# Feed-forward networks with nine paired blocks instead of eight, and way down's sums added to x by DMAs

## The chip, the cores and the metric

The kernel runs on one core of a Trainium2 chip. The metric is device time in microseconds (us), from a run of the whole program on that core; a smaller number is better. The span in a profile goes from the first to the last instruction of the program.

## The reference

One layer of a transformer: two feed-forward networks (FFNs) with a mixer of two kinds of attention between them, on 512 tokens of width 1024, all in float32.

```python
def rmsnorm(x, g):
    xf = x.astype(jnp.float32)
    y = xf * lax.rsqrt(jnp.mean(xf * xf, axis=-1, keepdims=True) + RMS_EPS)
    return (y * g.astype(jnp.float32)).astype(x.dtype)

def swiglu(h, w_gate, w_up, w_down):
    return (jax.nn.silu(h @ w_gate) * (h @ w_up)) @ w_down

def reference(x, ...):
    for l in range(DEPTH):          # DEPTH = 1
        x = x + 0.5 * swiglu(rmsnorm(x, norm_ffn1[l]), w_ffn1_gate[l], w_ffn1_up[l], w_ffn1_down[l])
        x = x + hybrid_mixer(rmsnorm(x, norm_mix[l]), ...)
        x = x + 0.5 * swiglu(rmsnorm(x, norm_ffn2[l]), w_ffn2_gate[l], w_ffn2_up[l], w_ffn2_down[l])
    return rmsnorm(x, norm_final)
```

The FFN's inner width is 2816, that is 22 blocks of 128 features.

## The kernel before

**Layout and precision.** x is kept transposed: xs[0] to xs[7], each 128 model rows by 512 tokens. TensorE (PE) takes every operand as two halves, hi and lo, whose sum is the float32 value: ACT copies the value into the rounded type (hi), DVE subtracts (lo). A product is three matmuls, hi hi, hi lo and lo hi (`mm3`, lines 93 to 95), summed in PSUM.

**An FFN.** Each of the 22 feature blocks needs gate and up (1024 x 128 each, times x) and gives a tile h = silu(gate) * up, again in halves (`kept`). Way down then multiplies the h tiles and adds half of the sum to xs[d], for the eight d.

- *Plain blocks* (`plain`), the first PLAIN = 6: the norm's gain is in x's halves (`gained`, tiles xo), 1/rms is not; R holds 1/rms as a 128 x 512 tile, and `finish` multiplies both sums by it. In three-block groups, the first half of x's rows (j = 0) comes for all blocks before the second.
- *Pairs* (`pair`), the other 16 blocks as 8 pairs: one Strassen-like scheme with seven products instead of eight, on halves of the tokens (HT = 256 columns) and of x's rows. Its operands on x's side are the blocks B11, B21, B22 and the sums T1 to T4, which `sums_of_x` and `blocks_of_x` form from x times gain times R while the plain blocks run; on the weights' side A11, A12, A22 and the sums S1 to S4 (DVE). Banks: u in tag s, v in t, w in o. When its last product ends, a closure (`c11`, `c12`, `c22`, `c21`) adds the banks, applies silu and keeps h.
- *Way down* (`down`) is cut into steps of three matmuls, called fills; its sums lie in the PSUM banks of tag mm (two of them). When a sum is complete, `half_added` (DVE, line 485) adds half of it to xs[d]. The h blocks form parts: the six plain ones, then fours. The fills of a part are mixed into the pair steps of the next part (`mixed`); the first LEAD = 12 fills of the plain part come at once after the plain blocks (`begun`).

**Order of the work.** `go` writes out PE's order by hand. A step has a cost, and loads, sums and halves are issued when PE is 26.0, 12.8 and 8.6 us of such cost away. The closures of a product are issued one step late. The other engines' orders, and PE's outside of `go` and of the mixer, are a planner's. Weights come in 512 KB loads on the SP queue: `raw` (three buffers) for plain blocks and way down, `aw` (six) for pairs; split weights are in sph and spl (three each).

**Beginning and end.** Twelve matmuls on ones (`wake`) run before the data are there. The first weight block is loaded in pieces and split at columns 2, 4 and 8. After the second FFN's pairs, `turn_x` transposes x (PE: px), first xs[0] to xs[3] for the four token blocks, then xs[4] to xs[7]; the last part's way down is formed per token block with h as the weights, and the final norm follows.

**The mixer** has its own order by hand; projections (pp) use the mm banks, logits (ps_s) the s banks. A small product, ps_c, comes four times and takes an mm bank.

Of the kernel before, what the change touches and what calls it, by code (L numbers as in the profile page):

```python
# [9 lines left out]
F32 = mybir.dt.float32  # L10
# [5 lines left out]
S = 512  # L16
# [5 lines left out]
FP = 4  # L22
PLAIN = 6
# [5 lines left out]
LEAD = 12  # L29
# [3 lines left out]
def block_kernel(ctx: ExitStack, tc: tile.TileContext, A: dict, out: bass.AP):  # L33
# [140 lines left out]

    class Ffn:


        def __init__(self, w, which, tmp, hp, sp):
            self.w, self.which, self.tmp, self.hp, self.sp = w, which, tmp, hp, sp
            self.xg, self.hs, self.early, self.cuts = None, {}, {}, ()  # L180
            self.b, self.temps = {}, {}
# [3 lines left out]
        def two(self, k):  # L185
            return [self.sp.tile([128, 2, 4, 128], F32, name=n, tag=t, bufs=3).rearrange("p a b c -> p (a b c)")
                    for n, t in (("xa", "sph"), ("xb", "spl"))]

        def sums_of_x(self, k):
            ac, bd = self.two(k)  # L190
            a, c, b, d = ac[:, :S], ac[:, S:S + HT], bd[:, :S], bd[:, S:]
            for t, i in ((a, k), (b, k + 4)):
                nc.vector.scalar_tensor_tensor(t, xs[i], gcol[:, self.which, i:i + 1], R, ALU.mult, ALU.mult)
            nc.vector.tensor_tensor(c, a[:, :HT], a[:, HT:], ALU.subtract)
            nc.vector.scalar_tensor_tensor(d[:, HT:], c, -1.0, b[:, HT:], ALU.mult, ALU.subtract)
            nc.vector.scalar_tensor_tensor(d[:, :HT], d[:, HT:], -1.0, b[:, :HT], ALU.mult, ALU.subtract)
            nc.vector.tensor_tensor(a[:, HT:], b[:, HT:], a[:, HT:], ALU.subtract)
            self.halves_of_x(self.th[:, k, 0:2], self.tl[:, k, 0:2], d.rearrange("p (a b) -> p a b", a=2))
            self.halves_of_x(self.th[:, k, 2], self.tl[:, k, 2], a[:, HT:])
            self.temps[k] = a[:, :HT], b, c  # L200
# [5 lines left out]
        def blocks_of_x(self, k):  # L206
            a, b, c = self.temps.pop(k)
            for i in (k, k + 4):
                self.b[i] = [xp.tile([128, S], F32R, name="xo", tag="xo", bufs=20) for _ in range(2)]
            hi, lo = self.b[k]  # L210
            self.halves_of_x(hi[:, :HT], lo[:, :HT], a)
            self.halves_of_x(hi[:, HT:], lo[:, HT:], c)
            self.halves_of_x(*self.b[k + 4], b)

        def moving(self, name):

            first, second = slice(0, HT), slice(HT, S)
            k, cols = {"B11": (0, first), "T1": (0, second), "B21": (4, first), "B22": (4, second)}.get(
                name, (None, None))
            if cols:  # L220
                return [(self.b[i][0][:, cols], self.b[i][1][:, cols]) for i in range(k, k + 4)]
            n = ("T4", "T2", "T3").index(name)
            return [(self.th[:, i, n], self.tl[:, i, n]) for i in range(4)]
# [4 lines left out]
        def kept(self, f, h):  # L228

            hi, lo = [self.hp.tile([128, S], F32R, name="h", tag="h", bufs=16) for _ in range(2)]  # L230
            nc.scalar.activation(hi, h, AF.Copy)
            nc.vector.tensor_tensor(lo, h, f32(hi), ALU.subtract)
            self.hs[f] = hi, lo

        def raw(self):
            return self.sp.tile([128, 2, 4, 128], F32, name="aw", tag="aw", bufs=6)

        def split(self, v):

            hi, lo = [self.sp.tile([128, 2, 4, 128], F32R, name=n, tag=n, bufs=3) for n in ("sph", "spl")]  # L240
            self.halves_of_x(hi, lo, v)
            return hi, lo

        def plain(self, fs):
# [3 lines left out]
            def loads(f, j):  # L248
                if (f, j) in self.early:
                    A[f, j] = self.early.pop((f, j))  # L250
                    return
                A[f, j] = chunk((8, 128))
                nc.sync.dma_start(A[f, j], self.w[f][:, j].rearrange("p a b c -> p (a b) c"))

            def halves_of(f, j):
                half[f, j] = halves(A.pop((f, j)), (2, 4, 8) if (f, j) in self.cuts else (8,))

            def run(f, j, m):
                if j == 0:
                    bank[f, m] = pt(("s", "t", "o", "mm")[(2 * f + m) % 4], "pgu")  # L260
                for k in range(4):
                    mm3(bank[f, m], half[f, j][4 * m + k], self.xg[4 * j + k], j == k == 0, j == 1 and k == 3)
# [16 lines left out]
        def pair(self, f):  # L279
# [3 lines left out]
            def loads(j):  # L283
                for i in range(2):
                    A[i, j] = self.raw()
                    nc.sync.dma_start(A[i, j], self.w[f + i][:, j])

            def sums(name):
# [4 lines left out]
                nc.vector.tensor_tensor(to, x, y, op)  # L293
# [7 lines left out]
            def run(m, n, to, a, b, first):  # L301
# [4 lines left out]
                for k, x in list(enumerate(self.moving(b)))[2 * n:2 * n + 2]:  # L306
                    mm3(bank[to][:, m], (hi[:, m, k], lo[:, m, k]), x, first and m == k == 0, k == 3, True)
# [16 lines left out]
            def c22():  # L324
                t = out[1] = self.t()
                nc.vector.tensor_tensor(t[:, :, HT:], bank["u"], part["w1"], ALU.add)
                nc.scalar.activation(t[:, 0, HT:], t[:, 0, HT:], AF.Silu, scale=-1.0)
                nc.vector.scalar_tensor_tensor(t[:, 1, HT:], t[:, 1, HT:], -1.0, t[:, 0, HT:], ALU.mult, ALU.mult)
# [58 lines left out]
        def mixed(self, steps, fills):  # L387

            out, done = [], 0
            ends, inner = range(5, len(steps) - 1, 2), range(6, len(steps) - 2, 2)  # L390
            more = max(0, len(fills) - len(ends))
            taken = set(ends[:len(fills)]) | {inner[(2 * n + 1) * len(inner) // (2 * more)] for n in range(more)}
            for i, s in enumerate(steps):
                out.append(s)
                if i in taken:
                    out.append(fills[done])
                    done += 1
            return out + fills[done:]
# [33 lines left out]
    def begun(ffn, w, first, posts):  # L432

        steps = [s for f in range(0, PLAIN, 3) for s in ffn.plain(range(f, f + 3))]
        sums = [(first + 2 * k, lambda k=k: ffn.sums_of_x(k)) for k in range(4)]
        blocks = [(at, lambda k=k: ffn.blocks_of_x(k)) for k, at in enumerate((first, 18, 18, 23))]
        for at, post in posts + sums + blocks:
            steps[at].post.append(post)
        fills = ffn.down(w, range(PLAIN), half_added, "mm", 2)
        return steps + fills[:LEAD], fills[LEAD:]  # L440

# [44 lines left out]

    with ExitStack() as ph:
# [6 lines left out]
        for _ in range(12):  # L494
# [5 lines left out]
        for f in range(3):  # L500
# [12 lines left out]
        first_w(0, [slice(0, 2)], nc.scalar)  # L513
        first_w(0, [slice(2, 4)], nc.sync)
# [5 lines left out]
        first_w(2, [slice(0, 8)], nc.sync)  # L520
# [8 lines left out]
        ffn.xg = [gained(k, 0) for k in range(NK)]  # L529

# [20 lines left out]
        def then(d, p):  # L551
# [4 lines left out]
        steps, fills = begun(ffn, A["wd1"], 6, [  # L556
            (3, squares_of_tokens), (4, lambda: roots(0, ss[:, 0])), (5, lambda: rows_of_roots(0, "mm")),
            (12, make_rows)])
        pairs = []
        for f in range(PLAIN, NF, FP):  # L560
            fs = range(f, f + FP)
            own = [step for i in fs[::2] for step in ffn.pair(i)]
            pairs += own
            steps += ffn.mixed(own, fills)
            if fs[-1] < NF - 1:
                fills = ffn.down(A["wd1"][f:], fs, half_added)
            else:
                steps += ffn.down(A["wd1"][f:], fs, then, None, 4)
        pairs[36].post.append(put_rows)
# [6 lines left out]
    with ExitStack() as ph:  # L576
# [411 lines left out]
        def cmp_pair(pair):  # L988
# [4 lines left out]
            def logits():  # L993
                need("kc")
                s = pt("mm", "ps_c")
# [140 lines left out]
    with ExitStack() as ph:  # L1136
# [7 lines left out]
        steps, fills = begun(ffn, A["wd2a"], 5, [  # L1144
            (2, lambda: roots(2, sums_of_squares("mm"))), (4, lambda: rows_of_roots(2, "mm"))])
        for f in range(PLAIN, NF, FP):
            fs = range(f, f + FP)
            steps += ffn.mixed([step for i in fs[::2] for step in ffn.pair(i)], fills)
            if fs[-1] < NF - 1:
                fills = ffn.down(A["wd2a"][f:], fs, half_added)  # L1150
        ffn.go(steps)
# [31 lines left out]
        last = range(NF - FP, NF)  # L1183
        w = []
        for half in range(2):
# [3 lines left out]
            hi, lo = [t.rearrange("p a b c -> p (a b c)") for t in ffn.split(v.rearrange("p (a b c) -> p a b c", a=2, b=4))]  # L1189
# [40 lines left out]
def _gate_up(gate, up):  # L1230
# [3 lines left out]
    return np.ascontiguousarray(v.transpose(4, 3, 1, 0, 2, 5))  # L1234


def _down(w):
# [4 lines left out]
    for f, end in zip((0, *range(PLAIN, NF, FP)), (*range(PLAIN, NF + 1, FP),)):  # L1242
# [5 lines left out]
def _laid_out(x, norm_ffn1, w_ffn1_gate, w_ffn1_up, w_ffn1_down, norm_mix, w_in, cmp_pos_k, cmp_w1_k,  # L1248
# [24 lines left out]
        "wd2a": _down(w_ffn2_down[0])[:NF - FP],  # L1273
        "wd2b": _blocks(w_ffn2_down[0][F - FP * 128:], FP * 128, S),
# [27 lines left out]
```

## Time and profile before

| | |
|---|---|
| median of 3 runs | 986.14 us (984.13 to 986.63) |
| profiled execution | 982.87 us, its span 981.0 us |
| granted TensorE clock, mean | 0.998 |
| PE, DVE, ACT, POOL busy | 970.0, 702.2, 499.0, 168.9 us |
| DMA | 113.86 MB, mean 116 GB/s |
| first FFN: first product starts, plain blocks end | 6.79, 74.23 us |
| second FFN: plain blocks end, pairs end | 695.5, 948.5 us |

A row of a group of instructions reads: line, engine, operation, tile written <- tiles read, shapes, count | busy us, mean ns of one | idle time of the engine before them, and what ended it. A timeline row reads: start us, duration us, engine, line, operation, tiles, shapes, count, and in brackets the idle time before it. A row of waits reads: who waited for whom: us in total, times, longest. A row of a stretch reads: from:to, its length, then busy time (and count) of PE, weight loads, DVE, ACT and POOL, granted clock, DMA share, GB/s. Matmuls overlap in the rows: the time of one is read from start to start.

### The profile page before, as it was taken

What the parts mean: (1) busy time and instruction counts of PE and PEld (TensorE: products, weight loads), DVE (VectorE), ACT (ScalarE), POOL (GpSimd) and SP (SyncE); (2) the same over time, 40 slices, a digit from 0 to 9 for tenths busy, and PEclk for the clock granted to TensorE, in tenths of its full rate; (3) what the DMA queues carried; (4) which work ended last, traced back from release to release, by engine and by line L of the source; (5) the groups of instructions that cost most, each with busy time, mean ns of one, the idle gap of its engine ahead of it and who ended that gap; (6) DMA issues with size and microseconds to landing.
All of it is one profiled execution on the core that took longest, in us unless ns stands there. A gap on an engine that the chain in (4) does not pass through costs nothing.

```text
span 981.0 us, 15636 instructions
## 1 busy us (share of the span) xinstructions
PE 970.0 (99%) x5944; PEld 857.6 (87%) x5944; DVE 702.2 (72%) x1118; ACT 499.0 (51%) x853; POOL 168.9 (17%) x297
## 2 busy tenths in 40 slices
PE   9999999999999999999999999999999999999997
PEld 7888989999999898888888888888899999999995
DVE  4996576878676475668878885688765777767653
ACT  7654344444434345577666674645443434434444
POOL 0000000000000144256566564800000000000002
PEclk9999999999999999999999999999999999999999
DMA  9633247332321135662233531543333233342102
GB/s 328 220 111 123 79 155 204 106 125 86 109 86 42 46 103 155 213 182 74 61 102 97 130 98 54 194 171 107 97 119 129 84 97 100 108 130 93 37 1 86
DMA packets 45742, 113.86 MB, mean 116 GB/s; under 512 B 10049, under 2 KB 14866, under 8 KB 45668
## 3 DMA queue, kind: packets, MB, share of 16 engines
q1 hardware_dynamic: 45380, 112.73, 37.0%
q8 instruction: 47, 0.77, 0.3%
q14 instruction: 27, 0.22, 0.1%
q10 hardware_dynamic: 288, 0.14, 0.1%
HBM read 100.08 MB, written 5.30 MB: 107 GB/s over the span
## 4 chain that ended last, share of the span: by engine, by line
PE 93%; DMA 2%; POOL 1%; DVE 1%; issue 1%; SPq 1%; ACT 0%; DVEq 0%; ACTq 0%; POOLq 0%
PE pd L94 8%; PE pd L95 8%; PE pd L93 8%; PE pu L93 6%; PE pu L95 6%; PE pu L94 6%; PE pw L93 4%; PE pw L95 4%; PE pw L94 4%; PE pgu L94 4%; PE pgu L95 4%; PE pgu L93 4%; PE pv L93 3%; PE pv L95 3%; PE pv L94 3%; PE pp L93 3%
## 5 line engine op out<-in xcount | busy, mean ns | idle before, releaser
L203 ACT ACTIVATE sph<-aw 128x1024 fp32r<-128x1024 f32 x114 | 121.0, 1061 | 222.5 <-PE pu L94 112.7
L81 ACT ACTIVATE whi<-raw 128x1024 fp32r<-128x1024 f32 (+3 forms) x115 | 112.2, 978 | 124.1 <-PE pd L94 50.4
L204 DVE TENSOR_TENSOR spl<-aw,sph 128x1024 fp32r<-128x1024 f32 x114 | 139.2, 1221 | 43.3 <-ACT sph L203 43.2
L88 DVE TENSOR_TENSOR wlo<-raw,whi 128x1024 fp32r<-128x1024 f32 (+3 forms) x90 | 111.2, 1237 | 37.5 <-ACT whi L81 36.6
L94 PE MATMUL pd<-h,whi 128*128 128x512 f32 x320 | 126.7, 396 | 0.0
L93 PE MATMUL pd<-h,whi 128*128 128x512 f32 x320 | 126.1, 394 | 0.0
L95 PE MATMUL pd<-h,wlo 128*128 128x512 f32 x320 | 125.8, 393 | 0.0
L95 PE MATMUL pu<-th,spl 128*128 128x256 f32 x384 | 106.2, 277 | 0.0
L93 PE MATMUL pu<-th,sph 128*128 128x256 f32 x384 | 106.1, 276 | 0.0
L293 DVE TENSOR_TENSOR aw<-aw 128x1024 f32<-128x1024 f32 x64 | 78.1, 1220 | 39.0 <-DMA aw<-in_wgu 32.3
L94 PE MATMUL pu<-tl,sph 128*128 128x256 f32 x384 | 106.0, 276 | 0.0
L93 PEld LDWEIGHTS pu<-th,sph 128*128 128x128 f32 x384 | 72.1, 188 | 6.4 <-issue 0.5
L94 PEld LDWEIGHTS pu<-tl,sph 128*128 128x128 f32 x384 | 72.1, 188 | 5.5
L93 PE MATMUL pgu<-xo,whi 128*128 128x512 f32 x192 | 75.4, 393 | 0.0
L94 PE MATMUL pgu<-xo,whi 128*128 128x512 f32 x192 | 74.9, 390 | 0.3 <-DVE xo L130 0.3
L95 PE MATMUL pgu<-xo,wlo 128*128 128x512 f32 x192 | 74.8, 389 | 0.0
L86 POOL TENSOR_TENSOR wlo<-raw,whi 128x128 fp32r<-128x128 f32 x136 | 64.1, 505 | 57.3 <-ACT whi L81 29.2
L95 PEld LDWEIGHTS pu<-th,spl 128*128 128x128 f32 x384 | 72.1, 188 | 0.0
L95 PEld LDWEIGHTS pd<-h,wlo 128*128 128x128 f32 x320 | 60.1, 188 | 13.4
L95 PE MATMUL pw<-xo,spl 128*128 128x256 f32 x256 | 70.8, 277 | 0.0
L93 PE MATMUL pw<-xo,sph 128*128 128x256 f32 x256 | 70.7, 276 | 0.0
L94 PE MATMUL pw<-xo,sph 128*128 128x256 f32 x256 | 70.7, 276 | 0.0
(253 smaller groups left out, 2423.0 us busy)
## 6 DMA issues: line engine op xcount, KB each, us to landing
aw<-in_wgu SPq DMA_DIRECT2D x64, 512.0 KB, 3.8
raw<-in_wgu SPq DMA_DIRECT2D x23, 512.0 KB, 5.3
raw<-in_wd SPq DMA_DIRECT2D x22, 512.0 KB, 3.5
raw<-in_wd2a SPq DMA_DIRECT2D x18, 512.0 KB, 3.6
raw<-in_w_a SPq DMA_DIRECT2D x16, 512.0 KB, 3.6
raw<-in_w SPq DMA_DIRECT2D x8, 512.0 KB, 3.9
kvn<-xo SPq DMA_DIRECT2D x32, 128.0 KB, 2.4
aq<-xo SPq DMA_DIRECT2D x32, 128.0 KB, 2.4
```

The costliest lines, as they stand in the source:

```text
L81: nc.scalar.activation(hi[:, s], src[:, s], AF.Copy)
L86: nc.gpsimd.tensor_tensor(lo[:, i, b], src[:, i, b], f32(hi[:, i, b]), ALU.subtract)
L88: nc.vector.tensor_tensor(lo[:, s], src[:, s], f32(hi[:, s]), ALU.subtract)
L93: nc.tensor.matmul(p, w[0], v[0], start=first, stop=False, skip_group_check=again)
L94: nc.tensor.matmul(p, w[0], v[1], start=False, stop=False, skip_group_check=again)
L95: nc.tensor.matmul(p, w[1], v[0], start=False, stop=last, skip_group_check=again)
L203: nc.scalar.activation(hi, v, AF.Copy)
L204: nc.vector.tensor_tensor(lo, v, f32(hi), ALU.subtract)
L293: nc.vector.tensor_tensor(to, x, y, op)
```

## The change

1. PLAIN = 4: four plain blocks in groups of two, then nine pairs. Parts of way down: 0-3, 4-5, 6-9, 10-13, 14-17, 18-21.
2. Pairs take x with its gain but without 1/rms: the blocks B are the plain blocks' own halves xo, `blocks_of_x` goes, and `sums_of_x` forms the T from x times gain (two ACT copies per row pair, four DVE operations, then halves). R multiplies the finished products: one DVE operation of 128 x 1024 in `c12` and one in `c21`; `c21` first copies its bank.
3. `half_sent` replaces `half_added` for all parts but the plain one, and there for odd d: ACT copies half of the sum to acc (one tile), and a DMA issued by POOL adds acc to xs[d].
4. `mixed`: a fill follows pair step i if i modulo 28 is in SLOTS (16 of 28) and the fill's part is at least six steps old; what is over comes after the last pair. LEAD = 10.
5. First block: gate and up of a 128-row piece are adjacent in memory and, for the block loaded in pieces, in PE's order; its first load is four columns on SP, a third early block is not loaded; 8 matmuls of wake instead of 12.
6. Order on the other engines: pair loads behind the last plain load on SP, sums S behind the last lo of h on DVE, the scaled x behind the last xo or h on ACT; the plain blocks' halves at high priority.
7. In the mixer, ps_c takes an s bank instead of an mm bank.

```diff
-FP = 4
-PLAIN = 6
+PLAIN = 4
+PARTS = (0, 4, 6, 10, 14, 18, 22)
-LEAD = 12
+LEAD = 10
+SLOTS = (0, 1, 2, 3, 4, 5, 6, 7, 9, 12, 15, 18, 21, 23, 25, 27)
...
         def sums_of_x(self, k):
...
-            for t, i in ((a, k), (b, k + 4)):
-                nc.vector.scalar_tensor_tensor(t, xs[i], gcol[:, self.which, i:i + 1], R, ALU.mult, ALU.mult)
...
+            with after(self.behind):
+                for n, i in enumerate((k, k + 4)):
+                    nc.scalar.activation(ab[:, n * S:(n + 1) * S], xs[i], AF.Copy, scale=gcol[:, self.which, i:i + 1])
+            a1, a2, b1, b2 = [ab[:, i * HT:(i + 1) * HT] for i in range(4)]
+            t4, t2, t3, t1 = [v[:, i] for i in range(4)]
+            nc.vector.tensor_tensor(t1, a1, a2, ALU.subtract)
+            nc.vector.scalar_tensor_tensor(t2, t1, -1.0, b2, ALU.mult, ALU.subtract)
+            nc.vector.scalar_tensor_tensor(t4, t2, -1.0, b1, ALU.mult, ALU.subtract)
+            nc.vector.tensor_tensor(t3, b2, a2, ALU.subtract)
+            self.halves_of_x(self.th[:, k], self.tl[:, k], v[:, :3])
...
-        def blocks_of_x(self, k):
...
+            def run(f, j, at):
+                both = (f, j) in self.cuts
+                order = [(k, m) for k in range(2 * at, 2 * at + 2) for m in range(2)] if both else [
+                    (k, at) for k in range(4)]
...
             def c12():
...
+                nc.vector.tensor_tensor(t, t, R.unsqueeze(1).to_broadcast([128, 2, S]), ALU.mult)
...
             def c21():
                 t = out[1]
-                nc.scalar.activation(t[:, 0, :HT], bank["u"][:, 0], AF.Silu, scale=-1.0)
-                nc.vector.scalar_tensor_tensor(t[:, 1, :HT], bank["u"][:, 1], -1.0, t[:, 0, :HT], ALU.mult, ALU.mult)
+                nc.scalar.activation(t[:, :, :HT], bank["u"], AF.Copy)
+                nc.vector.tensor_tensor(t, t, R.unsqueeze(1).to_broadcast([128, 2, S]), ALU.mult)
+                nc.scalar.activation(t[:, 0], t[:, 0], AF.Silu, scale=-1.0)
+                nc.vector.scalar_tensor_tensor(t[:, 1], t[:, 1], -1.0, t[:, 0], ALU.mult, ALU.mult)
                 self.kept(f + 1, t[:, 1])
...
         def mixed(self, steps, fills):
...
+                if i % 28 in SLOTS and fills and fills[0][0] <= i:
+                    out.append(fills.pop(0)[1])
+            return out + [fill for _, fill in fills]
...
+        steps = [s for f in range(0, PLAIN, 2) for s in ffn.plain(range(f, f + 2))]
+        sums = [(at, lambda k=k: ffn.sums_of_x(k)) for k, at in enumerate((3, 7, 9, 11))]
...
+        fills = ffn.down(w, range(PLAIN), lambda d, p: (half_sent if d % 2 else half_added)(d, p), "mm", 2)
+        return steps + fills[:LEAD], [(0, step) for step in fills[LEAD:]]
...
+    def half_sent(d, p):
+        nc.scalar.activation(acc, p, AF.Copy, scale=0.5)
+        nc.gpsimd.dma_start(xs[d], acc, accum_op=ALU.add)
...
-        for _ in range(12):
+        for _ in range(8):
...
         first_x(0)
-        first_w(0, [slice(0, 2)], nc.scalar)
-        first_w(0, [slice(2, 4)], nc.sync)
+        first_w(0, [slice(0, 4)], nc.sync)
         first_x(1)
...
-        first_w(2, [slice(0, 8)], nc.sync)
...
+        for f, end in zip(PARTS[1:], PARTS[2:]):
+            fs = range(f, end)
+            pairs += [step for i in fs[::2] for step in ffn.pair(i)]
+            if end < NF:
+                fills += [(len(pairs) + 6, step) for step in ffn.down(A["wd1"][f:], fs, half_sent)]
+        steps += ffn.mixed(pairs, fills) + ffn.down(A["wd1"][f:], fs, then, None, 4)
...
-                s = pt("mm", "ps_c")
+                s = pt("s", "ps_c")
```

The second FFN is put together as the first, without the group of four at its end.

More of the change, by code (lines that the diff above doesn't have):

```diff
@@ L173, in __init__, with after @@
             self.ahead, self.post = (loads, sums, halves), []
+    def after(ins):
+        return tc.issue_after(ins.ins if hasattr(ins, "ins") else ins)
     class Ffn:
@@ L180, in __init__ @@
             self.xg, self.hs, self.early, self.cuts = None, {}, {}, ()
[L181 removed]
+            self.behind = made[0]
+            self.t1 = [[xp.tile([128, S], F32R, name="xo", tag="xo", bufs=20) for _ in range(2)] for _ in range(2)]
             self.th, self.tl = [sp.tile([128, 4, 3, HT], F32R, name=n, tag=n, bufs=1) for n in ("th3", "tl3")]
             nc.gpsimd.memset(sp.tile([128, 16], F32, name="gap", tag="gap", bufs=1), 0.0)
[L185 to L187 removed]
@@ L197, in sums_of_x @@
[L197 to L200, printed above, removed]
+            ab, v = [self.sp.tile([128, 4, 2, 128], F32, name=n, tag=t, bufs=3).rearrange("p a b c -> p (a b c)")
+                     for n, t in (("xa", "sph"), ("xv", "spl"))]
+            v = v.rearrange("p (a b) -> p a b", a=4)
@@ L204, in halves_of_x @@
             nc.vector.tensor_tensor(lo, v, f32(hi), ALU.subtract)
-        def blocks_of_x(self, k):
[L207 to L213, printed above, removed]
-        def moving(self, name):
[L217 to L223, printed above, removed]
+        def moving(self, name):
+            if name == "T1":
+                return [[h[:, k % 2 * HT:(k % 2 + 1) * HT] for h in self.t1[k // 2]] for k in range(4)]
+            if name[0] == "T":
+                n = ("T4", "T2", "T3").index(name)
+                return [(self.th[:, i, n], self.tl[:, i, n]) for i in range(4)]
+            k, c = {"B11": (0, 0), "B21": (4, 0), "B22": (4, 1)}[name]
+            cols = slice(c * HT, (c + 1) * HT)
+            return [(self.xg[i][0][:, cols], self.xg[i][1][:, cols]) for i in range(k, k + 4)]
         def t(self):
@@ L252, in loads @@
                 A[f, j] = chunk((8, 128))
-                nc.sync.dma_start(A[f, j], self.w[f][:, j].rearrange("p a b c -> p (a b) c"))
+                self.behind_load = nc.sync.dma_start(A[f, j], self.w[f][:, j].rearrange("p a b c -> p (a b) c"))
             def halves_of(f, j):
[L256 to L262, printed above, removed]
+                with tc.high_priority():
+                    half[f, j] = halves(A.pop((f, j)), (2, 4, 8) if (f, j) in self.cuts else (8,))
+            def run(f, j, at):
+                both = (f, j) in self.cuts
+                order = [(k, m) for k in range(2 * at, 2 * at + 2) for m in range(2)] if both else [
+                    (k, at) for k in range(4)]
+                for k, m in order:
+                    if j == k == 0:
+                        bank[f, m] = pt(("s", "t", "o", "mm")[(2 * f + m) % 4], "pgu")
+                    mm3(bank[f, m], half[f, j][2 * k + m], self.xg[4 * j + k], j == k == 0, j == 1 and k == 3)
             def finish(f):
@@ L387, in mixed @@
         def mixed(self, steps, fills):
[L389 to L392, printed above, removed]
+            out, fills = [], list(fills)
             for i, s in enumerate(steps):
                 out.append(s)
[L395 to L398, printed above, removed]
+                if i % 28 in SLOTS and fills and fills[0][0] <= i:
+                    out.append(fills.pop(0)[1])
+            return out + [fill for _, fill in fills]
         def go(self, steps):
@@ L429, in go, with begun @@
                     late()
[L432 to L437, printed above, removed]
+    def begun(ffn, w, posts):
+        steps = [s for f in range(0, PLAIN, 2) for s in ffn.plain(range(f, f + 2))]
+        sums = [(at, lambda k=k: ffn.sums_of_x(k)) for k, at in enumerate((3, 7, 9, 11))]
+        for at, post in posts + sums:
             steps[at].post.append(post)
-        fills = ffn.down(w, range(PLAIN), half_added, "mm", 2)
-        return steps + fills[:LEAD], fills[LEAD:]
+        fills = ffn.down(w, range(PLAIN), lambda d, p: (half_sent if d % 2 else half_added)(d, p), "mm", 2)
+        return steps + fills[:LEAD], [(0, step) for step in fills[LEAD:]]
     scr_t = dp.tile([16, 128, RVW], F32, name="scr_t")
@@ L529, in block_kernel @@
         ffn.xg = [gained(k, 0) for k in range(NK)]
+        ffn.behind = made[0]
         def squares_of_tokens():
@@ L554, in then @@
             squares(tmp, d, "tmp", 3)
-        steps, fills = begun(ffn, A["wd1"], 6, [
+        steps, fills = begun(ffn, A["wd1"], [
             (3, squares_of_tokens), (4, lambda: roots(0, ss[:, 0])), (5, lambda: rows_of_roots(0, "mm")),
-            (12, make_rows)])
+            (13, make_rows)])
         pairs = []
[L560 to L569, printed above, removed]
+        for f, end in zip(PARTS[1:], PARTS[2:]):
[4 more added lines that the diff above has]
+        steps += ffn.mixed(pairs, fills) + ffn.down(A["wd1"][f:], fs, then, None, 4)
+        pairs[20].post.append(put_rows)
         for i in range(8):
@@ L1142, in block_kernel @@
         hs = ffn.hs
-        steps, fills = begun(ffn, A["wd2a"], 5, [
+        steps, fills = begun(ffn, A["wd2a"], [
             (2, lambda: roots(2, sums_of_squares("mm"))), (4, lambda: rows_of_roots(2, "mm"))])
[L1146 to L1151, printed above, removed]
+        pairs = []
+        for f, end in zip(PARTS[1:], PARTS[2:]):
+            fs = range(f, end)
+            pairs += [step for i in fs[::2] for step in ffn.pair(i)]
+            if end < NF:
+                fills += [(len(pairs) + 6, step) for step in ffn.down(A["wd2a"][f:], fs, half_sent)]
+        ffn.go(steps + ffn.mixed(pairs, fills))
         def turn_x(i, half):
@@ L1241, in _down @@
     chunks = []
-    for f, end in zip((0, *range(PLAIN, NF, FP)), (*range(PLAIN, NF + 1, FP),)):
+    for f, end in zip(PARTS, PARTS[1:]):
         part = v[:, :, f:end]
```

38 lines of the change are left out of this document (18 added, 20 removed).

## The prediction

> **What bounds the kernel now.** I read the page's busy times first, then its slices, then what PE waited for, then stretches of the FFNs.
>
> ```profile
> span 981.0 us, 15636 instructions
> PE 970.0 (99%) x5944; PEld 857.6 (87%) x5944; DVE 702.2 (72%) x1118; ACT 499.0 (51%) x853; POOL 168.9 (17%) x297
> PE   9999999999999999999999999999999999999997
> POOL 0000000000000144256566564800000000000002
> PE wake L495 <- DVE ones L113: 1.5, 1, 1.5
> PE ps_c L1000 <- DVE t L611: 1.0, 1, 1.0
> 13.47:74.23 60.76, 60.76 (x273) 50.45 (x272) 53.14 (x87) 37.50 (x60) 0.00 (x0) 1.00 0.59 205
> 703.60:948.50 244.90, 244.90 (x1741) 227.10 (x1741) 171.88 (x194) 104.14 (x134) 0.00 (x0) 1.00 0.30 93
> ```
>
> PE is the bound: it is busy in every slice but the last, and what it waits for is short (two rows of the longest waits stand above). In the stretch rows the columns after the length are busy time of PE, weight loads, DVE, ACT, POOL. In the first FFN's plain blocks (13.47 to 74.23) DVE is at 53.14 of 60.76, in the second FFN's pairs at 171.88 of 244.90: there is room, least in the plain stage. So time falls only if PE gets less to do, and every new wait of PE adds its full length. 0.3% of 986.14 is 3.0 us, about what a measurement of this kernel can tell from no change.
>
> **Nine pairs for eight, four plain blocks for six.** Durations of overlapping matmuls mislead, so I take starts.
>
> ```profile
> 68.11 0.39 PE L93 MATMUL pgu<-xo,whi 128*128 128x512 f32 x1
> 70.83 0.39 PE L93 MATMUL pgu<-xo,whi 128*128 128x512 f32 x1
> 947.18 0.28 PE L93 MATMUL pu<-th,sph 128*128 128x256 f32 x1
> 948.54 3.66 PE L1157 MATMUL px<-ident,x 128*128 128x128 f32 x32
> 951.95 0.48 PE L93 MATMUL pd<-whi,h 128*128 128x512 f32 x1
> ```
>
> From 68.11 to 70.83 twelve matmuls of 512 columns start: 2.72 us, 0.227 each. From 947.18 to 948.54 twelve of 256: 1.36 us, 0.113 each. Two plain blocks are 2 x 48 x 0.227 = 21.8 us, a pair is 7 x 24 = 168 x 0.113 = 19.0. Each FFN trades one for the other: -2.7, both -5.4 us. Way down keeps its matmuls.
>
> **What DVE and ACT get instead.**
>
> ```profile
> L293 DVE TENSOR_TENSOR aw<-aw 128x1024 f32<-128x1024 f32 x12 | 14.6, 1220 | 9.0 <-DMA aw<-in_wgu 9.0
> L485 DVE SCALAR_TENSOR_TENSOR x<-pd,x 128x512 f32<-128x512 f32 x14 | 9.6, 688 | 2.9 <-PE pd L95 2.9
> L311 ACT ACTIVATE wc<-pu 128x512 f32<-128x512 f32 x7 | 4.1, 579 | 0.0
> 936.66 1.23 DVE L204 TENSOR_TENSOR spl<-aw,sph 128x1024 fp32r<-128x1024 f32 x1 [0.95 <-ACT sph L203]
> 945.12 0.28 PE L93 MATMUL pu<-th,sph 128*128 128x256 f32 x1
> ```
>
> Per pair DVE gains two multiplications by R over 128x1024 (2 x 1.22) and loses four additions to x (4 x 0.69): -0.3 us. ACT gains four copies for the sends and one out of the bank, about 5 x 0.58 = 2.9 us; at 104.14 of 244.90 it has the room. Each h comes about 1.8 us later (1.22 + 0.58). A fill (way down's step of three matmuls, 0.68 us) uses it only from the sixth step of the next pair on, so this is hidden; without that cover it would cost 1.8 us once per part. Halves of weights stand ready early: the split of 936.66 ends 7.2 us before the product at 945.12, which hides a blocked ACT of that length. The sums of x lose eight multiplications by gcol and R and the halves of the blocks; all of that lay under PE in the plain stage, so I book nothing but relief for DVE there.
>
> **The start.** Eight wake-up matmuls instead of twelve; each 128-row piece of x now meets gate and up before the next piece; the second load is one of four columns on SP, and the third early block goes.
>
> ```profile
> 1.50 5.49 PE L495 MATMUL wake<-ones 128*128 128x512 f32 x12 [1.50 <-DVE ones L113]
> 5.30 0.72 ACT L81 ACTIVATE whi<-raw 128x256 fp32r<-128x256 f32 x2 [0.90 <-DMA raw<-in_wgu]
> 6.79 0.63 PE L93 MATMUL pgu<-xo,whi 128*128 128x512 f32 x1
> 7.57 0.39 PE L95 MATMUL pgu<-xo,wlo 128*128 128x512 f32 x1
> 7.79 0.39 PE L93 MATMUL pgu<-xo,whi 128*128 128x512 f32 x1
> 8.63 1.42 DVE L130 SCALAR_TENSOR_TENSOR xo<-x,gcol,xo 128x512 fp32r<-128x512 f32 x2
> 9.44 0.50 PE L94 MATMUL pgu<-xo,whi 128*128 128x512 f32 x1 [0.29 <-DVE xo L130]
> 13.47 0.39 PE L93 MATMUL pgu<-xo,whi 128*128 128x512 f32 x1
> ```
>
> Today the first 24 products run from 6.79 to 13.47. With both banks per piece the first six need only piece 0 and could start at about 6.2 (halves from 5.30 on, plus a weight load); pieces 2 and 3 are whole at 9.34 and 10.05 (the two of 8.63), so the 24 end at about 11.9: -1.6 us. Against it stands the clock: until about 7.5 matmuls start every 0.44 us (twelve between 1.50 and 6.79), from 7.57 on every 0.227, after 6.0 us of unbroken work. Eight wake-ups end at 1.50 + 8 x 0.44 = 5.0, and PE then idles 1.2 us. If the rate rises only 6.0 us after the restart, at 12.2, 13.6 products run slow and the rest take 2.4 us: end at 14.6, +1.1. Between -1.6 and +1.1 I take -0.3, as the gap is short beside the work before it.
> "TensorE: Matmul & The Clock Gate" of the Trainium skill (Part 1) says that the clock goes up after one busy window of about 3.4 us that runs freely. By that rule, counted from a restart at 6.2, the 24 would end at about 13.4, which is 0.0 to 0.1 us gained; the trace, with the rise 6.0 us after PE's first matmul, allows it.
>
> **Attention.** The small product ps_c moves from the banks of tag mm to those of tag s: its one wait of 1.0 us is for a DVE scaling that frees an mm bank. The s banks are read by DVE too, so between +1.0 and -1.0; I take -0.9, as the banks of s turn over with each step there.
>
> **From plain blocks to way down.** Ten of way down's fills follow at once, over four h instead of six.
>
> ```profile
> 74.01 0.39 PE L95 MATMUL pgu<-xo,wlo 128*128 128x512 f32 x1
> 78.52 0.68 DVE L232 TENSOR_TENSOR h<-t,h 128x512 fp32r<-128x512 f32 x1
> 81.91 1.37 DVE L485 SCALAR_TENSOR_TENSOR x<-pd,x 128x512 f32<-128x512 f32 x2 [1.58 <-PE pd L95]
> 695.27 0.39 PE L95 MATMUL pgu<-xo,wlo 128*128 128x512 f32 x1
> 700.72 0.69 DVE L232 TENSOR_TENSOR h<-t,h 128x512 fp32r<-128x512 f32 x1
> 694.07 0.75 DVE L204 TENSOR_TENSOR xo<-xa,xo 128x256 fp32r<-128x256 f32 x2
> 695.34 0.69 DVE L204 TENSOR_TENSOR xo<-xb,xo 128x512 fp32r<-128x512 f32 x1
> ```
>
> The last h is whole 5.0 us (74.23 to 79.20) and 5.9 us (695.50 to 701.41) after the last plain matmul. Today the tenth fill is the first to need it, 10 x 0.68 = 6.8 us on; now it is the seventh, after 6 x 0.68 = 4.1 us, its low half 0.2 later. With today's chains PE would wait 0.7 and 1.6 us. The ninth fill needs the bank of the first sum, freed by a DVE addition of 0.69 that has 0.68 us: about 0.3 each. Against that the halves of the blocks of x, which delayed DVE there (694.07 to 696.03), are gone. Bounds 0 and 4.0 us over both FFNs; I take +1.2.
>
> **Sums sent by DMA.** Per sum: ACT copies half the bank to acc (0.58), POOL issues a DMA that adds acc to x. POOL has nothing else then (zeros in its slices), and nothing queues there. There is one acc, so the next copy waits on ACT, with the halves of weights behind it, until the DMA has landed. No adding DMA is in this trace; the nearest rows:
>
> ```profile
> kvn<-xo SPq DMA_DIRECT2D x32, 128.0 KB, 2.4
> out<-xo SPq DMA_DIRECT2D x8, 256.0 KB, 2.3
> x<-in_xT SPq DMA_DIRECT2D x8, 256.0 KB, 4.4
> ```
>
> 256 KB takes 2.3 to 4.4 us; an addition reads its target as well, so I take 3.0. Sums follow each other every 5.4 us at the closest with four h, so nothing waits; with two h three follow at 2.7 us, and ACT falls 3 x (3.6 - 2.7) = 2.7 us behind, inside the 7.2 of cover: 0. The place that counts is the second FFN's end. By the slots, six fills stay over after the ninth pair; the last but one sum ends 1.36 us and the last 4.08 us after it. With landing time L the first send is down at 1.94 + L, the second copy then starts, and x7 is whole at 2.5 + 2L. PE ends the fills at 4.08 and the 16 transposes of x0 to x3 at 5.8 (32 took 3.41 us from 948.54 to 951.95), then needs x7: it waits 2L - 3.3 us. L = 2.3 gives 1.3, 4.4 gives 5.5, 3.0 gives 2.7. From there PE's order is not written out by hand; way down's last products of x's left half are ready, and a planner may put them first, which brings the lower bound to 0. I take +1.6.
>
> **Sum.** -5.4 - 0.3 - 0.9 + 1.2 + 1.6 = -3.8 us. The profiled execution took 982.87 us around a span of 981.0, 3.3 below the median of 986.14; it would take 979.1, the median 982.3.
>
> **Rivals.** (a) All of it hides: no wait at way down nor at x7: -6.6, 979.5. For it: the long leads of the splits; against: the two chains of h above, longer than their new cover.
> (b) The short plain stage binds: DVE, at 87% there, delays the last h, and the start stays cold: -5.4 + 1.1 + 4.0 - 0.9 + 1.6 = +0.4, 986.5. For it: 53.14 of 60.76; against: the work that goes from just there.
> (c) Slower by the round trip of the send: with L = 5.0 x7 makes PE wait 6.7, and the three close sums hold ACT 3 x (5.6 - 2.7) = 8.7, 1.5 over its cover in each FFN: -6.6 + 1.2 + 6.7 + 3.0 = +4.3, 990.4. It decides from L = 4.8 on. For it: no row shows an adding DMA; against: plain ones of that size land in 2.3.
> "SBUF — State Buffer" of the Trainium skill (the "DVE blocks DMA" trap) speaks for (c): descriptors of DMAs that POOL issues can't be written while DVE runs a two-port instruction. The page excepts tensor_tensor, and the FFN rows of DVE above are TENSOR_TENSOR and SCALAR_TENSOR_TENSOR; no row here tests it.
> (d) The pairs don't save, since PE waits for more splits: against it are the 7.2 us of lead; I give it almost nothing.
>
> **How the numbers follow.** Forecast 0.45 (979 to 985), (a) 0.20, (b) 0.20, (c) and (d) 0.15. Of the forecast's 0.45 some 0.30 lies below 983.2 and 0.15 above; (a) is faster; (b) is split, 0.15 same, 0.05 faster or slower. That gives faster 0.54, same 0.30, slower 0.16. The lower end, 977.0, takes the start's -1.6 and ps_c's -1.0 with all else hidden (978.1), and the 1.1 that runs differ by; the upper, 989.5, leaves out most of (c).
>
> **What would show it.** pu, pv and pw 9/8 as many, pgu two thirds; a wait of PE at px <- x by a DMA of 2 to 3 us, or pd before px; waits at pd <- h after the plain blocks of 1 us or less; the 14th to 24th product at 0.227; no wait at ps_c. The forecast is wrong if the sends land in 5 us, if PE waits for sph or spl in the third pair, or if the chains of h grow.

## The result, and the profile after

| | before | after |
|---|---|---|
| median of 5 runs | 984.13 us (983.01 to 986.63) | 996.25 us (994.09 to 997.28) |
| profiled execution, its span | 982.87, 981.0 us | 994.09, 992.0 us |
| first FFN, way down's last matmul starts | 350.42 us | 356.25 us |
| from there to the second FFN's first product (mixer) | 277.27 us long | 276.72 us long |
| second FFN, first product to the end of the span | 353.30 us long | 359.06 us long |

The ratio is 1.0122, 95% interval 1.0105 to 1.0140: slower by 1.2%, where 0.4% faster was forecast and 989.5 us was the upper end. The loss lies in the FFNs alone: each is 5.8 us longer, where nine pairs for eight should have made it 2.7 shorter, so about 8.5 us are lost in each. The page of the kernel after, its rows of busy time, of the queue that carries the sends, and of the sends themselves:

```profile
span 992.0 us, 16135 instructions
PE 968.3 (98%) x6084; PEld 861.9 (87%) x6084; DVE 705.7 (71%) x1054; ACT 556.2 (56%) x931; POOL 232.1 (23%) x369
q0 software_dynamic: 10368, 18.88, 11.4%
L489 POOL DMA_DIRECT2D x<-acc x72 | 62.7, 871 | 596.4 <-ACT acc L488 590.9
L488 ACT ACTIVATE acc<-pd 128x512 f32<-128x512 f32 x72 | 42.5, 590 | 59.1 <-DMA x<-acc 45.0
x<-acc POOLq DMA_DIRECT2D x72, 256.0 KB, 3.8
```

PE's work shrank as it should (970.0 to 968.3 us busy), but the span grew: PE now waits. The row of L488 says what for: the copies into acc cost ACT 42.5 us of work and 59.1 of idle time before them, 45.0 of it until the send before had landed. What PE waited for, and how long a send takes from its issue:

```profile
PE pd L94 <- ACT acc L488: 6.3, 2, 4.2
PE pu L94 <- ACT wc L315: 4.0, 2, 2.1
PE pd L94 <- DVE x L485: 1.8, 2, 0.9
```

```profile
DMA to landing us min/median/max: 3.3/3.8/8.7
```

No row of ps_c is left among the waits, and none of px. The waits for acc and wc lie in two places: the stretch of the second and third pair in each FFN, where the fills of the *two-block part* (blocks 4 and 5, the first pair's h) are mixed in. With two h a sum is complete after two fills instead of four. ACT there, in the first FFN:

```profile
114.69 0.60 ACT L488 ACTIVATE acc<-pd 128x512 f32<-128x512 f32 x1 [2.75 <-DMA x<-acc]
120.96 0.60 ACT L488 ACTIVATE acc<-pd 128x512 f32<-128x512 f32 x1 [1.89 <-DMA x<-acc]
121.97 0.59 ACT L335 ACTIVATE t<-pu 128x512 f32<-128x512 f32 x1
128.97 0.60 ACT L488 ACTIVATE acc<-pd 128x512 f32<-128x512 f32 x1 [5.49 <-DMA x<-acc]
133.38 0.60 ACT L488 ACTIVATE acc<-pd 128x512 f32<-128x512 f32 x1 [1.91 <-DMA x<-acc]
133.88 0.59 ACT L315 ACTIVATE wc<-pu 128x512 f32<-128x512 f32 x1
138.52 0.60 ACT L488 ACTIVATE acc<-pd 128x512 f32<-128x512 f32 x1 [2.16 <-DMA x<-acc]
143.02 0.60 ACT L488 ACTIVATE acc<-pd 128x512 f32<-128x512 f32 x1 [2.00 <-DMA x<-acc]
```

Every copy of this part, eight in each FFN, starts when the send before has landed, 4.4 to 8.0 us after the copy before. The slots would bring sums 2.7 to 5.4 us apart. The wc copies, which empty the pairs' banks, stand in ACT's order behind acc. PE at the worst place, and the clock there in stretches:

```profile
125.11 0.28 PE L96 MATMUL pu<-xo,spl 128*128 128x256 f32 x1
129.62 0.50 PE L94 MATMUL pd<-h,whi 128*128 128x512 f32 x1 [4.23 <-ACT acc L488]
130.44 0.42 PE L94 MATMUL pu<-xo,sph 128*128 128x256 f32 x1
130.65 0.42 PE L95 MATMUL pu<-xo,sph 128*128 128x256 f32 x1
```

```profile
125.11:129.70 4.59, 0.36 (x4) 0.17 (x2) 0.56 (x1) 0.73 (x2) 0.00 (x0) 1.00 0.39 98
130.40:133.80 3.40, 3.40 (x14) 3.07 (x13) 3.28 (x4) 1.05 (x2) 0.43 (x1) 0.50 0.44 77
133.80:137.20 3.40, 3.40 (x25) 3.13 (x24) 1.75 (x2) 2.56 (x4) 0.86 (x1) 1.00 0.46 79
```

After a wait of 4.2 us the granted clock is 0.50 for 3.4 us: products of 256 columns start every 0.215 us instead of 0.113, and 14 matmuls run where 25 do in the next 3.4 us. So the wait costs about 1.7 us more than its own length. In the second FFN the same part makes PE wait three times, until 739.49, 756.51 and 767.72, the last time for 2.06 us, and then:

```profile
768.70:772.10 3.40, 3.40 (x18) 3.40 (x18) 2.31 (x2) 0.41 (x1) 0.00 (x0) 0.50 0.88 230
```

The wait until 756.51 was as long, 2.03 us, and no half clock followed. Waits and half clocks of this part, counted as what lies between two starts beyond the usual step, sum to 8.3 us in the first FFN and 6.9 in the second.

### The profile page after: what moved, and what is told of

It reads as the page before. It is cut to its first block, busy times and chain, and to the rows that moved or that the text cites. A ratio compares the mean times of both kernels' runs of the same rounds, so it can differ in the third digit from the quotient of the medians.

```text
span 992.0 us, 16135 instructions
## 1 busy us (share of the span) xinstructions
PE 968.3 (98%) x6084; PEld 861.9 (87%) x6084; DVE 705.7 (71%) x1054; ACT 556.2 (56%) x931; POOL 232.1 (23%) x369
## 3 DMA queue, kind: packets, MB, share of 16 engines
q0 software_dynamic: 10368, 18.88, 11.4%
## 4 chain that ended last, share of the span: by engine, by line
PE 69%; issue 24%; POOL 3%; DMA 2%; ACT 1%; DVE 1%; SPq 0%; POOLq 0%; ACTq 0%; DVEq 0%
PE pd L95 6%; PE pd L96 6%; PE pd L94 6%; PE pu L94 5%; PE pu L96 5%; PE pu L95 5%; PE pw L94 3%; PE pw L95 3%; PE pw L96 3%; PE pp L94 3%; PE pp L96 3%; PE pp L95 3%; PE ps_t L963 3%; PE pv L96 2%; PE pv L94 2%
## 5 line engine op out<-in xcount | busy, mean ns | idle before, releaser
L210 DVE TENSOR_TENSOR spl<-aw,sph 128x1024 fp32r<-128x1024 f32 x128 | 155.1, 1222 | 99.3 <-ACT sph L209 97.0
L209 ACT ACTIVATE sph<-aw 128x1024 fp32r<-128x1024 f32 x128 | 133.7, 1058 | 147.0 <-PE pu L95 90.6
L489 POOL DMA_DIRECT2D x<-acc x72 | 62.7, 871 | 596.4 <-ACT acc L488 590.9
L94 PE MATMUL pu<-th,sph 128*128 128x256 f32 x432 | 120.3, 278 | 4.0 <-ACT wc L315 4.0
L96 PE MATMUL pu<-th,spl 128*128 128x256 f32 x432 | 120.1, 278 | 0.0
L95 PE MATMUL pu<-tl,sph 128*128 128x256 f32 x432 | 120.1, 278 | 0.0
L96 PEld LDWEIGHTS pu<-th,spl 128*128 128x128 f32 x432 | 81.9, 190 | 0.0
L94 PE MATMUL pw<-xo,sph 128*128 128x256 f32 x288 | 79.7, 277 | 0.5 <-ACT wc L315 0.5
L95 PE MATMUL pw<-xo,sph 128*128 128x256 f32 x288 | 79.5, 276 | 0.0
L488 ACT ACTIVATE acc<-pd 128x512 f32<-128x512 f32 x72 | 42.5, 590 | 59.1 <-DMA x<-acc 45.0
L94 PEld LDWEIGHTS pd<-h,whi 128*128 128x128 f32 x320 | 60.2, 188 | 11.9 <-ACT acc L488 6.8
```

The costliest lines, as they stand in the source:

```text
L94: nc.tensor.matmul(p, w[0], v[0], start=first, stop=False, skip_group_check=again)
L95: nc.tensor.matmul(p, w[0], v[1], start=False, stop=False, skip_group_check=again)
L96: nc.tensor.matmul(p, w[1], v[0], start=False, stop=last, skip_group_check=again)
L209: nc.scalar.activation(hi, v, AF.Copy)
L210: nc.vector.tensor_tensor(lo, v, f32(hi), ALU.subtract)
L488: nc.scalar.activation(acc, p, AF.Copy, scale=0.5)
```

## The experiments

Theory A: the two-block part's sums come closer together than one acc and an adding send can turn over; ACT, which works in order, is held, and PE with it. Rival B: the 72 sends cost by their traffic and POOL's time, wherever they lie. Rival C: the pairs themselves, with two multiplications by R and more copies, keep DVE and ACT too busy. The runs were spread over several chips, so each ratio below is to the kernel before on the same chip, whose median there lay between 982.73 and 984.22 us.

**Each of the two-block part's sums gets its own buffer** (kernel after, edited):

```
+    def half_sent_own(ffn, d, p):
+        a = ffn.hp.tile([128, S], F32, name="own", tag="h", bufs=16)
+        nc.scalar.activation(a, p, AF.Copy, scale=0.5)
+        nc.gpsimd.dma_start(xs[d], a, accum_op=ALU.add)
...
-  ffn.down(A["wd1"][f:], fs, half_sent)
+  ffn.down(A["wd1"][f:], fs, (lambda d, p: half_sent_own(ffn, d, p)) if len(fs) == 2 else half_sent)
(wd2a alike)
```

> The changed kernel, but each of the eight sums of the two-block part (4-5) is copied to a buffer of its own instead of acc; as many DMAs, the same bytes. Theory A (one acc: from the copy's start to the DMA's landing 4.7 us in the median, up to 9.6, against sums 2.7 to 5.4 us apart; ACT is held, mm banks and the copies wc come late): the waits in the second and third pair go, 8.3 us in the first FFN and 6.9 in the second with the slow clock behind them, so about 981 to 983 us. Rival B (the traffic of the added DMAs makes the weights late): nothing changes, 995 to 997. Rival C (nine pairs with R on the products keep ACT and DVE too busy): nothing changes, 995 to 997.

982.29 us, ratio 0.9992 (0.9977 to 1.0007). Waits on ACT and PE in it:

```profile
ACT acc L488 <- DMA x<-acc: 8.5, 7, 2.7
```

```profile
PE pd L94 <- ACT own L493: 2.1, 4, 0.6
PE pu L94 <- DVE t L331: 1.8, 2, 0.9
PE pd L94 <- DVE x L485: 1.7, 2, 0.9
```

Same sends, same number, same engine; only the wait for the one buffer is gone, and 1.3% of the time with it. The sends from own buffers even land later (median 6.2 us from issue), but nobody waits for them. A's number; B and C, which left the time near 996, fall.

**The two-block part's sums added by DVE** (`half_added if len(fs) == 2 else half_sent` at both places).

> The changed kernel, but the two-block part's sums are added to x by DVE as before; the other 56 sums are sent. Theory A: 981 to 984 us, as in the run with own buffers. Rival B: 16 of 72 DMAs less, so about a fifth of 12 us: 993 to 994. Rival C: 995 to 997.

982.54 us, ratio 0.9992 (0.9978 to 1.0006): the same cure from the other side, as A expected.

**All 72 sums added by DVE** (`half_added` at every place).

> The changed kernel with all sums added by DVE. Theory A: as with the two-block part alone, 981 to 984 us, since the other sends cost nothing. Rival B: all of the traffic goes, 978 to 982, clearly below the kernel that sends 56. Rival C: 995 to 997 or more, as DVE has 72 additions of 0.69 us more.

982.35 us, ratio 0.9990 (0.9974 to 1.0005), equal to the one above. The 56 sends of the plain part and of the four-block parts cost nothing and bring nothing. B falls a second time.

**The kernel before, with the sends of the 48 sums of its four-block parts** (`half_sent` for `half_added` at both places where parts are mixed).

> The kernel before, with the sums of its four-block parts but the last (48 sums, some 8 us apart) sent by DMAs through one acc; nothing else changed. Theory A: the round trip is shorter than the distance of the sums, no wait: within 2 us of the kernel before. Rival B: 48 of 72 DMAs of the changed kernel, so +6 to +9 us.

985.54 us, ratio 1.0012 (0.9995 to 1.0029). The copies start 5.3 to 10.3 us apart in each FFN, ACT still waits 22.4 us for landings, but PE never waits for acc: sends at that distance are harmless there too.

**Fills spread evenly** (kernel after; `SLOTS = (0, 2, 4, 6, 7, 9, 11, 13, 14, 16, 18, 20, 21, 23, 25, 27)`).

> The changed kernel with the 16 slots of a pair spread evenly (0, 2, 4, 6, 7, 9 ... 27) instead of dense at its start; the two-block part's sums are then 3.4 to 4.1 us apart instead of 2.7 to 5.4, the four-block parts' all 7.5 us. One acc, all sends kept. Theory A (one acc, round trip 4.7 us in the median): each sum still falls behind by about 1 us, eight of them by 8, little over the cover; the 15 us of waits shrink to 2 to 7: 984 to 989 us. Rival B (traffic) and rival C (ACT and DVE too busy over the whole pair): as before, 994 to 997.

999.85 us, ratio 1.0164 (1.0147 to 1.0181): a miss, the expectation had 984 to 989. The waits:

```profile
PE pd L94 <- ACT acc L488: 9.4, 6, 5.0
PE pu L94 <- DVE t L331: 3.1, 2, 1.6
```

Two reasons offer themselves after the fact; neither was tried alone. Spread evenly, the sums follow each other at 3.4 to 4.1 us, all eight closer than the shortest round trip (3.3 us of landing and 1.0 from the copy's start to the issue), so a late landing is never made good: one took 8.3 us (issued at 115.51), the next copy stood 7.82 us for it, and PE 4.96. And even slots cost by themselves, as a run below shows.

**The two-block part moved to the end** (`PARTS = (0, 4, 8, 12, 16, 18, 22)`).

> The changed kernel with the two-block part moved from second place (blocks 4-5) to last but one (16-17); parts 0-3, 4-7, 8-11, 12-15, 16-17, 18-21. Theory A: the waits move with it, from the second and third pair to the eighth and ninth, and stay about as long, 10 to 16 us in both FFNs: 990 to 998, with none in the second and third pair. Rival D (it is the beginning of the pairs that costs, while the loads and the sums of x catch up): the waits stay in the second and third pair.

1010.16 us, ratio 1.0275 (1.0251 to 1.0299), longer than either theory had. What PE waited for:

```profile
PE pu L94 <- DVE t L331: 9.2, 2, 8.7
PE pd L94 <- ACT acc L488: 7.4, 3, 3.2
PE px L1158 <- DMA x<-acc: 3.9, 2, 2.0
```

```profile
119.77 1.23 DVE L297 TENSOR_TENSOR aw<-aw 128x1024 f32<-128x1024 f32 x1 [9.95 <-DMA aw<-in_wgu]
```

The waits for acc moved with the part: they now end at 339.62, 344.04 and 348.45 us in the first FFN and at 974.18 and 978.48 in the second, the latter two for x itself, as A says and C can't. The rest is new: DVE stood 9.95 us for a load in the second pair, and PE 8.69. D's sign, a wait in the second pair, thus shows too, but for a load and not for acc. With ten steps of that pair now free of fills, it may have run ahead of its weights; but in the second FFN the same pair waits only 0.54 us (until 757.66), and there the small loads (cb) that stand between the weight loads on the SP queue of the first FFN are missing. Which of the two it takes was not tested. In the trace the wait of 8.69 us and the half clock behind it (0.50 until 127.59, some 3 us more) make about 12 us; the waits for acc and for x sent from it, 7.4 and 3.9 us, with the half clocks behind three of them make about 16, which is A's share.

**What keeps the gain from showing?** With the sends cured the kernel stood at 982.4, 1 us under the 983.4 of the kernel before on that chip, not 5.4. Two waits remain: the ninth of the ten fills that follow the plain blocks at once waits for the bank of the first sum (`PE pd <- DVE x L485`, 1.8 in total), and in the second and third pair PE waits for spl (1.5). DVE has hardly a gap there; the stretch in the second FFN, in the run with the two-block part's sums on DVE:

```profile
738.00:757.00 19.00, 18.92 (x137) 17.51 (x137) 18.18 (x22) 9.17 (x12) 0.00 (x0) 1.00 0.13 36
```

Eight fills at once instead of ten (`LEAD = 8`), with the two-block part's sums on DVE:

> Two-block part added by DVE, and 8 instead of 10 fills at once after the plain blocks, so that the ninth fill no longer waits for the bank of the first sum (1.0 us in each FFN). Theory A with the bank's wait as the next term: 1.5 to 2.5 us less than with 10, about 980. If the two fills only meet another wait: as with 10, 982.5.

**978.56 us, ratio 0.9948 (0.9934 to 0.9963)**: faster than both kernels, and a larger step than expected. From 0.9992 with ten fills it is 0.44%, 4.3 us, where 1.5 to 2.5 were expected: not only the bank's wait is gone, but that for spl too. Its longest waits:

```profile
PE wake L499 <- DVE ones L114: 1.5, 1, 1.5
PE ps_t L963 <- DVE tl L967: 0.7, 4, 0.2
PE pd L95 <- DVE h L230: 0.6, 1, 0.6
```

After the wake-ups no single wait of PE is longer than 0.6 us. That the wait for spl would go was not foreseen, and why it went was not tested. In its trace the first FFN's way down ends 2.7 us earlier than before (347.71 against 350.42), the mixer is 1.05 shorter and the second FFN 0.75.

**The same with even slots.**

> As the one before, with the slots spread evenly. With the two-block part added by DVE, DVE had no gap in the second and third pair (eight additions within 22 us) and PE waited there some 1.7 us in each FFN; spread out these should go: 977 to 979 us, 0.4 to 0.7% below the kernel before, the first version that beats it clearly. If DVE isn't what held: as the one before.

984.64 us, ratio 1.0014 (1.0002 to 1.0025): a miss by 6 us, with no send involved that differs from the run above.

```profile
PE pu L96 <- DVE spl L210: 4.1, 2, 2.0
```

PE waits for halves of weights. Why even slots make DVE late was not tested.

**Own buffers with `LEAD = 8`.**

> The changed kernel with own buffers for the two-block part's sums and 8 fills at once after the plain blocks: all 72 sums still go by DMA. Theory A: without the one acc the sends cost nothing, so as the kernel with that part added by DVE and 8 fills, 978 to 980 us. Rival B (traffic): 2 us or more above that one.

986.92 us, ratio 1.0038 (1.0025 to 1.0051): a miss too; 978 to 980 was expected. ACT there:

```profile
122.56 0.63 ACT L337 ACTIVATE t<-t 128x512 f32<-128x512 f32 x1 [1.11 <-DVE t L336]
124.83 1.06 ACT L209 ACTIVATE sph<-aw 128x1024 fp32r<-128x1024 f32 x1 [1.64 <-DVE aw L297]
126.32 1.07 ACT L493 ACTIVATE own<-pd 128x512 f32<-128x512 f32 x2
```

Two sums wait at once (x2), and PE, which needs their mm banks, stands 2.4 us (6.6 in four waits over the run). No DMA is in this chain: the copy stands in ACT's order behind a step of a closure (t, 122.56) and the hi half of a weight (sph, 124.83), both waiting for DVE. With the fills two slots further on, the sums meet the closure of the second pair. A sum that leaves its bank by ACT inherits ACT's waits; by DVE, which had those very instructions to do, it doesn't. This is read from the trace, not tried by a run of its own. By its number alone this run is what rival B expected (2 us or more above the run with DVE's additions); what speaks against B here is only that chain. That sends with own buffers cost nothing is thus shown for `LEAD = 10` alone; with 8 the sixteen cost some 9 us, by the ratios of this run and of the next one.

**Twelve wake-up matmuls instead of eight**, in the 978.56 kernel.

> The kernel with the two-block part added by DVE and 8 fills, with 12 wake-up matmuls instead of 8. If the wake-ups only stand in the first products' way: first product at 6.8 instead of 5.4 us, the first 24 end 0.4 to 1.3 us later, time +0.5 to +1.3. If 8 are too few for the clock: the first 24 end no later and the time is the same or less.

977.85 us, ratio 0.9950 (0.9932 to 0.9967): no difference. The first product starts at 6.20 instead of 5.55 us, but the 25th at 12.23 against 12.32: in both the 14th product waits for a piece of x (xo, 0.18 and 0.28 us), which takes up the lead.

**What makes the round trip long?** One run each, of the kernel after with the addition left out: the DMA overwrites x with the half sum. First issued by POOL as before, then by SP.

```
-        nc.gpsimd.dma_start(xs[d], acc, accum_op=ALU.add)
+        nc.gpsimd.dma_start(xs[d], acc)        (then: nc.sync.dma_start(xs[d], acc))
```

> The changed kernel with sums sent by a plain DMA on POOL: x is overwritten with half of the sum instead of added to. The price of a send by itself. If the addition (a second read of x) makes the round trip: landing at its shortest falls from 3.3 to about 2.3 us, as plain stores of 256 KB take, and the waits shrink by a third or more, to 985 to 992. If the issue on POOL and the landing itself make it: 3.0 to 3.3 us, time as the changed kernel.

> The same plain DMA (x overwritten) issued on SP. If POOL's issue is what is long: landing at its shortest 2.3 us, the round trip from the copy's start 3.3 instead of 4.2. Its waits can't be compared as a whole, since the weight loads stand behind each send on SP: I expect more waits for weights, 995 us or more.

On POOL 982.23 us, on SP 989.29 (the kernel before has a median of 982.73 in 14 runs on that chip). Both are below what was expected (985 to 992, and 995 or more). The rows on POOL:

```profile
q0 software_dynamic: 5760, 18.88, 5.1%
L489 POOL DMA_DIRECT2D x<-acc x72 | 39.0, 541 | 601.0 <-ACT acc L488 595.3
x<-acc POOLq DMA_DIRECT2D x72, 256.0 KB, 2.6
```

For the same 18.88 MB the addition costs 0.33 us more of POOL per issue (871 against 541 ns), 1.1 to 1.2 us more until it lands (2.2 at the shortest and 2.6 in the median, against 3.3 and 3.8), and more than twice the share of the DMA engines (11.4% against 5.1%). Without it the round trip is 3.2 us at the shortest, ACT's waits for it shrink from 45.0 to 13.5 us, and PE's wait for acc disappears. On SP the sends land in 2.3 us in the median and the time is worse all the same, since sends and loads stand in one queue there. At the worst place the copy of 100.12 was done at 100.7, but its send was issued at 106.69, behind 15 small loads (cb); the next two copies waited 6.37 and 4.50 us, and PE 2.8 us for the wc behind them.

## Why the prediction was wrong, point by point

The step that failed is the booking of the two-block part's sums: "with two h three follow at 2.7 us, and ACT falls 3 x (3.6 - 2.7) = 2.7 us behind, inside the 7.2 of cover: 0". In the trace it came to 15.2 us of waits and half clock; the cured kernels are 1.3%, some 13 us, faster by the ratios. None of the signs that the prediction named for being wrong came: the sends landed in 3.8 us in the median, and PE waited neither for sph or spl nor for h. Four things were wrong in it:

- *The size.* L was taken as 3.0; it was 3.3 at the shortest, 3.8 in the median and 8.7 at the longest, the long ones where other loads kept the DMA engines busy (a share of 0.98 beside the longest, from 88.70 to 98.40). The 0.6 of the copy was in the sum, the 0.4 us from the copy's end to POOL's issue was not. The round trip is 4.3 us at the shortest and 4.7 in the median, instead of 3.6. This alone would not have changed the booking: 3 x (4.7 - 2.7) = 6.0 is still inside 7.2.
- *The count.* Three sums were put in the queue. The others come at up to 5.4 us, hardly more than the round trip, so the backlog is never worked off; one landing of 6.9 us (copy at 120.96, the next at 128.97) is paid almost in full.
- *The cover.* 7.2 us was the lead of halves of weights, and the halves were indeed not what PE waited for. What PE waited for stands in the same ACT order with no such lead: the two mm banks, emptied by acc itself, and the pairs' banks, emptied by wc.
- *What a wait costs.* It was priced at its length. The wait of 4.23 us and one of 2.06 were each followed by 3.4 us at half clock, 1.7 us more.

Rival (c) had the right mechanism and the right sign, at a chance of at most 0.15: the round trip, and ACT held by close sums. It put most of its price, 6.7 us, on x7 at the end and 3.0 on the close sums, and set its threshold at L = 4.8; the close sums decided at L = 3.8, and x7 cost nothing. Its row against (plain copies land in 2.3 us) was true and beside the point: a plain copy measured 2.2 to 2.6 here, an adding one 3.3 to 3.8.

The other terms:

- *Nine pairs for eight, -5.4.* The arithmetic of products holds: the plain blocks end 22.5 us earlier in the first FFN and the plain stage is 22.2 shorter in the second, 21.8 being due. But less of it arrives: with the sends cured, the two FFNs save 3.5 us with `LEAD = 8` (2.7, the start's gain in it, and 0.75) and none with 10 (+0.2 and +0.8 us in the profiled execution with the two-block part's sums on DVE, itself 2.8 us above that kernel's median). By the ratio the kernel with 8 gains 5.1 us in all, with the start and the mixer. The remainder went into waits for the first sum's bank and for spl, so the supplies of DVE in the second and third pair were less ample than the stretch over all pairs (171.88 of 244.90) made them look. Rival (d) was right in kind, small in size.
- *The start, -0.3.* The products began at 5.09, right behind the eighth wake-up, with no idle 1.2 us, and 24 of them ended at 12.29 instead of 13.47: -1.2, within the bounds given. At the end of the plain blocks 0.7 of it was left.
- *ps_c, -0.9.* The wait is gone, as booked, but the mixer is only 0.55 us shorter after, with a wait of 1.2 us that was not there before (ps_t <- POOL lpn), and 1.05 in the fastest kernel, where that wait is 0.5.
- *From plain blocks to way down, +1.2.* It measured about 2.1 (1.03 in each FFN from start to start, 0.9 of it in the rows of waits), by the bank of the first sum, for which 0.3 each had been booked; the chains of h, which had the larger share, made no wait.
- *x7 at the end, +1.6.* None: the planner put the 16 transposes of x0 to x3 into the last pair, at 943.19, and way down's products ahead of the others. The lower bound of 0, given for that reason, held.
- *The sends of all other sums, 0.* Right: with and without them the time is the same (0.9992 and 0.9990).

Why the clock fell after one wait of about 2 us and not after another can be read from the trace of the kernel after. The changes of its granted clock lie whole multiples of 3.413 us apart: from the rise at 7.50 to the fall at 130.38 there are 36, from the rise at 133.80 to the fall at 768.68 there are 186. Cut at these times, the windows before the two falls in the FFNs, and one that a wait of 2.03 us reached into without a fall, read:

```profile
126.97:130.38 3.41, 0.76 (x3) 0.67 (x4) 0.27 (x1) 1.12 (x2) 0.41 (x1) 1.00 0.13 28
765.26:768.68 3.42, 1.36 (x12) 1.16 (x11) 1.25 (x2) 3.04 (x5) 0.86 (x1) 1.00 0.90 313
755.02:758.44 3.42, 1.93 (x11) 1.74 (x12) 1.26 (x2) 2.58 (x4) 0.88 (x1) 1.00 0.05 10
```

The clock fell where PE was busy for 0.76 and 1.36 us of a window, and stayed where it was busy for 1.83 or more: the waits of 1.91 and 2.03 us lie across two windows each. "TensorE: Matmul & The Clock Gate" of the Trainium skill (Part 1) says that such a window of about 3.4 us runs freely, and that the clock is at half rate after at least one idle window. The trace agrees with the first; with the second it differs, since neither window was idle throughout.

"DMA: Bandwidth & Descriptors" of the Trainium skill (Anatomy of one DMA — SWDGE (gpsimd) path) gives 2.0 us and bytes over 436 GB/s for a DMA issued by POOL, which is an estimate of 2.6 us for 256 KB; the plain sends agree with a median of 2.6, the adding ones, 3.8, do not.

## What to carry to other kernels

A sum that leaves by way of a DMA holds its staging buffer for the whole round trip: copy, issue and landing, which for an adding DMA took 3.8 us here, against 2.6 for a plain one. Compare that with the closest spacing of the buffer's users, not with their mean, and ask what stands behind the waiting copy on its engine; a buffer of its own for each sum of the one part that comes too close, or additions by DVE for that part, was worth 1.3% here, with ten fills at once. Cover is counted for what is really waited for: a long lead of one product of an engine (weights) says nothing of the others (banks) in the same order.

## What the runs showed of the hardware

- An adding DMA of 256 KB from SBUF to SBUF, issued by POOL: 0.87 us of POOL, 3.3 us to landing at the shortest, 144 packets, against 0.54 us, 2.2 us and 80 packets without the addition.
- Landing times have a long tail: 8.7 us in the kernel after, and a median of 6.2 where several sends from own buffers were under way at once.
- Waits of PE of 4.23 and 2.06 us in dense work were followed by 3.4 us at half clock, then by full clock at once; two others, of 1.91 and 2.03 us, were not. In the kernel after, the clock changed only at ends of windows of 3.413 us, and in the windows before these two falls PE was busy for 0.76 and 1.36 us.
- DVE, busy for 72% of the span, was not seen to hold up the plain sends from POOL: their issue took 536 ns in the median and 730 at the most, and they landed in 2.2 us at the shortest, as sends from SP did (2.3).
